# Second layer's u and gate projections: the hi weights meet hi and lo activations in one 512-column product

## The chip, the cores and the metric

One core of a Trainium2 chip runs the whole program. The metric is the device time of one execution in microseconds (us), as the median of several runs. TensorE (PE) does the matrix products, and the loads of its stationary operand are shown apart as PEld. VectorE (DVE), ScalarE (ACT) and GpSimd (POOL) do the elementwise work, and the queues of SyncE (SP) and ACT issue the DMAs.

## What is computed

Two residual layers over 256 positions of width 2048. The first is a bidirectional RWKV-7 mixer and is untouched here. The second is a gated spatial unit; cut to what matters:

```python
def chunked_sgu_mixer(h, w_in, ln_g, ln_b, w_s, b_s, w_out):
    u, v, gate = jnp.split(h @ w_in, 3, axis=-1)      # h: 256 x 2048, each part 4096 wide
    u = jax.nn.gelu(u)
    v = layer_norm(jax.nn.gelu(v), ln_g, ln_b)
    vc = v.reshape(Bsz, T // CHUNK, CHUNK, G_GROUPS, G_GROUP_W)
    s = jnp.einsum('gij,bcjgd->bcigd', w_s, vc) + b_s.T[:, :, None]
    s = s.reshape(Bsz, T, BRANCH)
    return (u * s * jax.nn.silu(gate)) @ w_out
```

The result is added to the input, and a final RMS norm closes the trunk.

## The kernel before

Every large product is made of three products of the type fp32r: both operands are split into a rounded part (hi) and the rest (lo), and hi·hi, hi·lo and lo·hi are summed in PSUM; lo·lo is left out. The function `mm3` (lines 159 to 163) issues the three: line 161 takes the first operand's hi and the second's hi, line 162 hi and lo, line 163 lo and hi.

Weights come from HBM in pieces of 128 x 1024 (512 KB). `convert` (lines 129 to 148) issues the DMA on SP's queue into a raw tile, ACT casts it to hi (line 146), and DVE subtracts to get lo (line 147). There are three hi and three lo tiles, so piece n+3 can be cast only when PE is through with piece n. `fetch` keeps up to three pieces converted ahead. The order in which each engine then runs its instructions is set by a scheduler when the program is built, from the program order and a simulated timeline.

The second layer has three stages:

- the v stage (lines 1008 to 1023): stationary are 128 x 128 blocks of the activations z1, moving are 512 columns of weights;
- the stage of u and gate, 16 groups of 256 channels (the loop from line 1033): here the weights are stationary and the activations move. For each of 16 k-blocks and 2 channel blocks `project` (lines 175 to 188) calls `mm3` with 256 columns (all positions): 192 products a group, 96 for u and 96 for gate. u and gate have one PSUM bank each (`ua`, `ga`), with both channel blocks side by side;
- the output stage (lines 1069 to 1095), with stationary blocks of the gated result (`zh_o1`, `zl_o1`, `bh_o1`, `bl_o1`) and 512 moving columns of weights. Its last eight pieces lie in tiles called `end`, which take over the place of z1.

In the group loop DVE multiplies the accumulated u by the RMS factor `rb2` (line 1041) and ACT takes its gelu (line 1042); DVE multiplies the gate likewise (line 1045), ACT takes a tanh into `Gt` (line 1046), DVE makes the SiLU from it (line 1047), and POOL multiplies it into U (line 1048). `Ga` and `Gt` have one buffer each. DVE also normalises the v columns of the group (lines 1055 to 1057), PE mixes them by four 128-column products (`sgu`, line 1061), and DVE and ACT put the result together and split it (lines 1063 to 1065 and `halve`). PSUM banks are handed out by `bank` (lines 791 to 793) in pairs, in turn from the tags acc and pg, with two banks each.

Of the kernel before, what the change touches and what calls it, by code (L numbers as in the profile page):

```python
# [11 lines left out]
F32R = mybir.dt.float32r  # L12
AF = mybir.ActivationFunctionType
ALU = mybir.AluOpType
# [8 lines left out]
def trunk(tc, x, norm_g, final_norm_g, w_in, mu_prev, mu_next, w0, w_up, a0, a_up, k_k, k_a, r_k,  # L23
          ln_w, ln_b, w_out, g_w_in, g_ln_g, g_ln_b, g_w_s, g_b_s, g_w_out, out):
    nc = tc.nc
    V, S, G, PE = nc.vector, nc.scalar, nc.gpsimd, nc.tensor
    P = 128
    T = x.shape[1]
    D = x.shape[2]
    KT = D // P  # L30
# [25 lines left out]
    def sm(name, tag="pg", bufs=2):  # L56
        return psm.tile([P, 512], F32, tag=tag, name=name, bufs=bufs)
# [92 lines left out]
    def prefetch():  # L150
        while queue and len(ready) < 3:
            ready.append(convert(*queue.popleft()))

    def fetch():

        prefetch()
        return ready.popleft()

    def mm3(acc, a, b, first, last):

        PE.matmul(acc, a[0], b[0], start=first, stop=False, skip_group_check=True)  # L161
        PE.matmul(acc, a[0], b[1], start=False, stop=False, skip_group_check=True)  # L162
        PE.matmul(acc, a[1], b[0], start=False, stop=last, skip_group_check=True)  # L163

    def run(steps):
        for _ in steps:
            pass
# [7 lines left out]
    def project(width, accs, zT):  # L175


        m = width // len(accs)
        k = 0
        while k < KT:  # L180
            n, hi, lo = fetch()
            for j in range(n):
                for i, acc in enumerate(accs):
                    cs = slice(i * m, (i + 1) * m)
                    mm3(acc, (hi[:, j, cs], lo[:, j, cs]), (zT[0][:, k], zT[1][:, k]),
                        k == 0 and i % 2 == 0, k == KT - 1)
                k += 1
                yield

# [19 lines left out]
    with tc.tile_pool(name="pr", bufs=6) as pr:  # L209
        groups, cur, n = [], [], 0  # L210
        for name, a in plist:
            if n + a.shape[0] > P:
                groups.append(cur)
                cur, n = [], 0
# [3 lines left out]
        for gi, grp in enumerate(groups):  # L218
            if gi == 1:
                prefetch()  # L220
            n = sum(a.shape[0] for _, a in grp)
# [47 lines left out]
    for k in range(DK, KT, 4):  # L269
        cs = slice(k * P, (k + 4) * P)  # L270
# [64 lines left out]
    for todo in plan:  # L335
        for s, b in todo:
# [3 lines left out]
            else:  # L340
                want_cols(w_in, segment[s] + b * 2 * P, 2 * P, f"w{s}{b}_")
    run(project(NL * P, laccs, zT))

    def low_rank():
# [70 lines left out]
    def mains(todo, st):  # L415
        slot = dict(k=0, r=4, g=12, v=8) if "k" in dict(todo) else dict(v=0, g=4)
        last = -4
        for s, b in todo:
            if s == "u":
                st[b]["wu"] = fetch()  # L420
                continue
            last = max(last + 4, slot[s])
            yield last * MT
            acc = acc_pair(f"acc{s}{b}")
            for i, _ in enumerate(project(2 * P, [acc[:, 0], acc[:, 1]], zT)):
                yield last * MT + i * dt
            if s == "g":
                SG = fr.tile([P, 2, T], F32, tag="SG", name=f"SG{b}", bufs=2)
                S.activation(SG, acc, AF.Tanh, scale=0.5)
                V.scalar_tensor_tensor(SG, SG, 1.0, acc, ALU.add, ALU.mult)  # L430
                st[b]["SG"] = SG
            elif s == "v":
                Vt = fr.tile([P, 2, T], F32, tag="Vt", name=f"Vt{b}", bufs=2)
                shifted(acc, Vt, b, 2)
                st[b]["Vt"] = Vt
            else:
                t = fr.tile([P, 2, T], F32, tag=f"{s}t", name=f"{s}t{b}")
                shifted(acc, t, b, dict(r=0, k=1)[s])
                st[b][dict(r="Rt", k="Kt")[s]] = t
        if ("g", NB - 1) in todo:  # L440
            yield 12 * MT
            for i, _ in enumerate(early_first()):
                yield 12 * MT + i
# [347 lines left out]
    def bank(name):  # L791
        banks[0] += 1
        return sm(name, ("acc", "pg")[(banks[0] - 1) // 2 % 2])

    def out_banks(m, name):
        return [bank(f"{name}{m}_{tt}") for tt in range(TT)]

    def halve(o, e0, n, src):

        S.mul(o[0][:, e0:e0 + n], src, 0.5)  # L800
        V.scalar_tensor_tensor(o[1][:, e0:e0 + n], src, 0.5, o[0][:, e0:e0 + n].bitcast(F32), ALU.mult, ALU.subtract)
# [100 lines left out]
    hp = top.enter_context(tc.tile_pool(name="hp", bufs=1, reuse_waits="tile"))  # L902
# [14 lines left out]
    ends = []  # L917

    def end_tiles(i):

        if not ends:
            ends.extend(hp.tile([P, KT, T], F32R, tag=f"z1{t}", name=f"end{t}").rearrange("p k t -> p (k t)")
                        .rearrange("p (e m) -> p e m", m=512) for t in "hl")
        return [t[:, 2 * i:2 * i + 2] for t in ends]

    wv = g_w_out.rearrange("(e p) m -> p e m", p=P)
    for i in range(LAST // 2):
        e = NCT - LAST + 2 * i
        want(wv[:, e:e + 2, (NM - 1) * 512:NM * 512], 2, 512, f"pe{e}", partial(end_tiles, i))
# [10 lines left out]
        o = oA if e < HE else oB  # L940
        return [t[:, e % HE:e % HE + n] for t in o]

    z1 = [hp.tile([P, KT, T], F32R, tag=f"z1{t}", name=f"z1{t}") for t in "hl"]
    part1 = hp.tile([P, TT, NM], F32, name="part1")
    def residual(m):

# [38 lines left out]
    rb2 = rb.unsqueeze(1).to_broadcast([P, 2, T])  # L985
# [17 lines left out]
    def vcols(tt, c, n):  # L1003
        return vn[c // (E // 2)][:, tt, c % (E // 2):c % (E // 2) + n]
# [3 lines left out]
    for n in range(nst):  # L1008
        accs = out_banks(n, "vacc")
        k = 0  # L1010
        while k < KT:
            m, hi, lo = fetch()
# [15 lines left out]
    V.tensor_scalar(vrs, vmv[:, :, 1], LN_EPS, None, ALU.add)  # L1028
    G.tensor_tensor(vrs, vrs, halfpow[:, :TT], ALU.pow)

    pA = [zp.tile([P, HE, T], F32R, tag=t, name=f"{t}_o1") for t in ("zh", "zl")]
    pB = None
    for g in range(NG):
        if g == NG // 2:
            pB = [op.tile([P, HE, T], F32R, tag="bh", name="bh_o1"), hp.tile([P, HE, T], F32R, name="bl_o1")]
        U = gt.tile([P, 2, T], F32, tag="U", name=f"U{g}")
        Ga = gt.tile([P, 2, T], F32, tag="Ga", bufs=1, name=f"Ga{g}")
        Gt = gt.tile([P, 2, T], F32, tag="Gt", bufs=1, name=f"Gt{g}")
        ua = bank(f"uacc{g}").rearrange("p (i t) -> p i t", i=2)
        run(project(256, [ua[:, 0], ua[:, 1]], z1))  # L1040
        V.tensor_tensor(U, ua, rb2, ALU.mult)
        S.activation(U, U, AF.Gelu_apprx_tanh)
        ga = bank(f"gacc{g}").rearrange("p (i t) -> p i t", i=2)
        run(project(256, [ga[:, 0], ga[:, 1]], z1))
        V.tensor_tensor(Ga, ga, rb2, ALU.mult)
        S.activation(Gt, Ga, AF.Tanh, scale=0.5)
        V.scalar_tensor_tensor(Gt, Gt, 1.0, Ga, ALU.add, ALU.mult)
        G.tensor_tensor(U, U, Gt, ALU.mult)
        gb = gt.tile([P, 2, 256], F32, tag="gb", name=f"gb{g}")
        nc.scalar.dma_start(gb[:, 0], g_ln_g[0, g * 256:(g + 1) * 256].partition_broadcast(P))  # L1050
        nc.scalar.dma_start(gb[:, 1], g_ln_b[0, g * 256:(g + 1) * 256].partition_broadcast(P))
        with tc.issue_after(latest[0].ins), tc.issue_after(latest[1].ins):
            for tt in range(TT):
                vs = vcols(tt, g * 256, 256)
                V.tensor_scalar(vs, vs, vmv[:, tt, 0:1], vrs[:, tt:tt + 1], ALU.subtract, ALU.mult)
                V.tensor_tensor(vs, vs, gb[:, 0], ALU.mult)
                V.tensor_tensor(vs, vs, gb[:, 1], ALU.add)
        sp = sm(f"sgu{g}", ("pf", "pq")[g % 2], 1).rearrange("p (n i) -> p n i", i=P)
        for cl in range(2):
            for tt in range(TT):  # L1060
                PE.matmul(sp[:, cl * TT + tt], vcols(tt, g * 256 + cl * P, P), wsT[:, g], start=True, stop=True)
        s1 = gt.tile([P, 4, P], F32, tag="s1", bufs=1, name=f"s1_{g}")
        V.tensor_tensor(s1, sp, bsb[:, g:g + 1].to_broadcast([P, 4, P]), ALU.add)
        V.tensor_tensor(s1, s1, U.rearrange("p l (t i) -> p (l t) i", i=P), ALU.mult)
        halve(pA if g < NG // 2 else pB, 2 * g % HE, 2, s1.rearrange("p (l t) i -> p l (t i)", l=2))
# [3 lines left out]
    for m in range(NM):  # L1069
        accs = out_banks(m, "oacc1_")  # L1070
# [9 lines left out]
        for tt in range(TT):  # L1080

            ts_ = slice(tt * P, (tt + 1) * P)
            for e in range(e1, NCT):
                oh, ol = o1(e)
                _, hi, lo = rest[(e - e1) // 2]
                mm3(accs[tt], (oh[:, ts_], ol[:, ts_]), (hi[:, e % 2], lo[:, e % 2]), e == 0, e == NCT - 1)
        parts = 1 if m < NM - 1 else 2
        for tt in range(TT):
            for i in range(parts):
                cs = slice(i * (512 // parts), (i + 1) * (512 // parts))  # L1090
# [5 lines left out]
    for tt in range(TT):  # L1096
        rstd2 = rms(total(part2[:, tt:tt + 1], f"ssq2_{tt}", hp), f"rstd2_{tt}", hp, V)
        for m in range(NM):
            h = h1[m][:, tt]
# [37 lines left out]
```

## Time and profile before

| what | value |
|---|---|
| median of 3 runs | 2262.61 us (2259.36 to 2264.06) |
| the profiled execution's own time | 2260.96 us |
| its span, first to last instruction | 2259.2 us |
| PE busy, PEld busy | 2210.5 us (98%), 2013.8 us (89%) |
| DVE, ACT, POOL busy | 1601.3 us (71%), 1389.6 us (62%), 197.4 us (9%) |
| chain that ended last | PE 80%, ACT 8%, DVE 4%, DMA 4%, waits for nothing shown 2% |
| mean granted TensorE clock | 0.992 of full speed |

The duration of a matmul row is its whole way through the array. Matmuls overlap, so what a product costs in a dense stretch is the distance between the starts of two that follow each other, read from the timeline.

### The profile page before, as it was taken

How to read it: one execution, taken by the hardware profiler on the slowest of the kernel's cores; microseconds unless marked ns; L12 is line 12 of the kernel's file. 1: busy time of each engine (PE TensorE's matmuls, PEld its weight loads, DVE VectorE, ACT ScalarE, POOL GpSimd, SP SyncE). 2: the span in 40 equal slices, each digit the busy share in tenths (PEclk: the TensorE clock that was granted, in tenths of full speed). 3: DMA queues.
4: the chain of work that ended last, by engine and by line, in shares of the span. 5: the costliest groups of instructions: out<-in, count | busy, mean ns of one | idle time of the engine just before them, and what ended most of it. 6: DMA issues, size and time to landing. Idle time of an engine off the chain costs nothing.

```text
span 2259.2 us, 50510 instructions
## 1 busy us (share of the span) xinstructions
PE 2210.5 (98%) x21008; PEld 2013.8 (89%) x21008; DVE 1601.3 (71%) x3057; ACT 1389.6 (62%) x2128; POOL 197.4 (9%) x230
## 2 busy tenths in 40 slices
PE   7999999999999999999999999999999999999998
PEld 7898899999999999999999977878889999999886
DVE  5798789778877977887797774465556676676444
ACT  6657777777868777786877774464444444444343
POOL 2220101011111101001110100000000000000000
PEclk9999899999999999999999999999999999999999
DMA  5444234343343344434333455576776666665554
GB/s 167 133 131 136 65 114 123 97 126 117 101 134 107 110 119 125 118 102 130 107 116 117 145 175 171 194 250 193 222 206 188 186 185 189 187 187 189 199 194 156
DMA packets 286135, 339.36 MB, mean 150 GB/s; under 512 B 11600, under 2 KB 233552, under 8 KB 285776
## 3 DMA queue, kind: packets, MB, share of 16 engines
q1 hardware_dynamic: 265648, 314.88, 45.9%
q10 hardware_dynamic: 20256, 21.24, 3.2%
q8 instruction: 165, 2.70, 0.5%
q14 instruction: 66, 0.54, 0.1%
HBM read 329.78 MB, written 6.29 MB: 149 GB/s over the span
## 4 chain that ended last, share of the span: by engine, by line
PE 80%; ACT 8%; DVE 4%; DMA 4%; issue 2%; POOL 0%; SPq 0%; ACTq 0%; POOLq 0%; DVEq 0%
PE oacc L162 4%; PE oacc L163 4%; PE oacc L161 4%; PE gp L557 4%; PE accv L161 3%; PE accg L161 3%; PE uacc L161 3%; PE gacc L163 3%; PE gacc L161 3%; PE gacc L162 3%; PE uacc L162 3%; PE uacc L163 3%; PE accg L163 3%; PE accg L162 3%; PE vacc L163 3%; PE vacc L162 3%
## 5 line engine op out<-in xcount | busy, mean ns | idle before, releaser
L161 PE MATMUL accv<-zh,whi_wv 128*128 128x256 f32 x512 | 153.4, 300 | 2.2 <-ACT whi_wv L146 2.2
L163 PE MATMUL accg<-zh,wlo_wg 128*128 128x256 f32 x512 | 151.3, 295 | 0.5 <-DVE wlo_wg L147 0.5
L161 PE MATMUL acck<-zh,whi_wk 128*128 128x256 f32 x512 | 150.4, 294 | 1.2 <-ACT whi_wk L146 1.2
L163 PE MATMUL acck<-zh,wlo_wk 128*128 128x256 f32 x512 | 148.7, 290 | 2.8 <-DVE wlo_wk L147 2.8
L163 PE MATMUL accv<-zh,wlo_wv 128*128 128x256 f32 x512 | 148.8, 291 | 1.3 <-DVE wlo_wv L147 1.2
L163 PE MATMUL accr<-zh,wlo_wr 128*128 128x256 f32 x512 | 149.2, 291 | 0.6 <-DVE wlo_wr L147 0.6
L162 PE MATMUL accr<-zl,whi_wr 128*128 128x256 f32 x512 | 148.7, 290 | 0.0
L161 PE MATMUL accr<-zh,whi_wr 128*128 128x256 f32 x512 | 148.3, 290 | 0.0
L161 PE MATMUL accg<-zh,whi_wg 128*128 128x256 f32 x512 | 148.0, 289 | 0.0
L162 PE MATMUL accv<-zl,whi_wv 128*128 128x256 f32 x512 | 147.3, 288 | 0.0
L162 PE MATMUL acck<-zl,whi_wk 128*128 128x256 f32 x512 | 147.2, 287 | 0.0
L162 PE MATMUL accg<-zl,whi_wg 128*128 128x256 f32 x512 | 146.4, 286 | 0.0
L162 PE MATMUL uacc<-z1l,whi_u 128*128 128x256 f32 x512 | 146.1, 285 | 0.0
L163 PE MATMUL uacc<-z1h,wlo_u 128*128 128x256 f32 x512 | 146.0, 285 | 0.0
L161 PE MATMUL uacc<-z1h,whi_u 128*128 128x256 f32 x512 | 144.9, 283 | 0.0
L161 PE MATMUL gacc<-z1h,whi_g 128*128 128x256 f32 x512 | 144.9, 283 | 0.0
L162 PE MATMUL gacc<-z1l,whi_g 128*128 128x256 f32 x512 | 144.9, 283 | 0.0
L163 PE MATMUL gacc<-z1h,wlo_g 128*128 128x256 f32 x512 | 144.9, 283 | 0.0
L146 ACT CAST whi_g<-raw_g 128x1024 fp32r<-128x1024 f32 x64 | 67.1, 1048 | 114.0 <-PE uacc L162 73.7
L147 DVE TENSOR_TENSOR wlo_v<-raw_v,whi_v 128x1024 fp32r<-128x1024 f32 x64 | 78.4, 1225 | 80.4 <-ACT whi_v L146 80.4
L610 DVE TENSOR_TENSOR TD<-La,X 128x126 f32<-128x126 f32 (+22 forms) x496 | 126.8, 256 | 10.5
L147 DVE TENSOR_TENSOR wlo_u<-raw_u,whi_u 128x1024 fp32r<-128x1024 f32 x64 | 93.8, 1465 | 56.6 <-ACT whi_u L146 56.6
(333 smaller groups left out, 7307.3 us busy)
## 6 DMA issues: line engine op xcount, KB each, us to landing
raw_wk<-in_rwkv_w_in_dram SPq DMA_DIRECT2D x64, 512.0 KB, 3.9
raw_wr<-in_rwkv_w_in_dram SPq DMA_DIRECT2D x64, 512.0 KB, 3.7
raw_wv<-in_rwkv_w_in_dram SPq DMA_DIRECT2D x64, 512.0 KB, 3.7
raw_wg<-in_rwkv_w_in_dram SPq DMA_DIRECT2D x64, 512.0 KB, 3.7
raw_o<-in_rwkv_w_out_dram SPq DMA_DIRECT2D x64, 512.0 KB, 4.0
raw_v<-in_gmlp_w_in_dram SPq DMA_DIRECT2D x64, 512.0 KB, 4.3
raw_u<-in_gmlp_w_in_dram SPq DMA_DIRECT2D x64, 512.0 KB, 3.6
raw_g<-in_gmlp_w_in_dram SPq DMA_DIRECT2D x64, 512.0 KB, 3.6
```

The costliest lines, as they stand in the source:

```text
L146: latest[0] = S.copy(hi, raw)
L147: latest[1] = V.tensor_tensor(lo, raw, hi.bitcast(F32), ALU.subtract)
L161: PE.matmul(acc, a[0], b[0], start=first, stop=False, skip_group_check=True)
L162: PE.matmul(acc, a[0], b[1], start=False, stop=False, skip_group_check=True)
L163: PE.matmul(acc, a[1], b[0], start=False, stop=last, skip_group_check=True)
L557: PE.matmul(gp[h][:, c].rearrange("p q t -> p (q t)"), BK[H[h], d, cl, c].rearrange("p q t -> p (q t)"), AR[H[h], d, cl, c].rearrange("p q ...
L610: V.tensor_tensor(tv, La[:, j, 0:j].unsqueeze(2).to_broadcast([P, j, n]), X[:, j:j + 1, m:].to_broadcast([P, j, n]), ALU.mult)
```

## The change

The hi and lo parts of z1 lie side by side in one tile `zc` of shape (128, 16, 2, 256), at the place and in the room that the two tiles had. A new `project_wide` takes, for each k-block and channel block, one 512-column product of the hi weights with hi and lo activations (line 200 of the changed kernel) and one 256-column product of the lo weights with the hi activations (line 202). Each channel block gets a PSUM bank of its own: the left half sums hi·hi and lo·hi, the right half hi·lo. At the end `gated` copies the right half to `tmp` (= `Gt`) on ACT, adds the left half on DVE, and multiplies by `rb2`. The v stage and the end tiles use views of the new tile.

```diff
+    def project_wide(width, accs, zc):
+        m = width // len(accs)
+        k = 0
+        while k < KT:
+            n, hi, lo = fetch()
+            for j in range(n):
+                for i, acc in enumerate(accs):
+                    cs = slice(i * m, (i + 1) * m)
+                    PE.matmul(acc.rearrange("p h t -> p (h t)"), hi[:, j, cs], zc[:, k].rearrange("p h t -> p (h t)"),
+                              start=k == 0, stop=False, skip_group_check=True)
+                    PE.matmul(acc[:, 0], lo[:, j, cs], zc[:, k, 0], start=False, stop=k == KT - 1,
+                              skip_group_check=True)
+                k += 1
+                yield
...
-    z1 = [hp.tile([P, KT, T], F32R, tag=f"z1{t}", name=f"z1{t}") for t in "hl"]
+    zc = hp.tile([P, KT, 2, T], F32R, tag="z1", name="z1")
+    z1 = [zc[:, :, i] for i in range(2)]
...
+    def gated(name, dst, tmp):
+        acc = [bank(f"{name}_{i}").rearrange("p (h t) -> p h t", h=2) for i in range(2)]
+        run(project_wide(256, acc, zc))
+        for i in range(2):
+            S.copy(tmp[:, i], acc[i][:, 1])
+            V.tensor_tensor(dst[:, i], acc[i][:, 0], tmp[:, i], ALU.add)
+        V.tensor_tensor(dst, dst, rb2, ALU.mult)
...
-        ua = bank(f"uacc{g}").rearrange("p (i t) -> p i t", i=2)
-        run(project(256, [ua[:, 0], ua[:, 1]], z1))
-        V.tensor_tensor(U, ua, rb2, ALU.mult)
+        gated(f"uacc{g}", U, Gt)
         S.activation(U, U, AF.Gelu_apprx_tanh)
-        ga = bank(f"gacc{g}").rearrange("p (i t) -> p i t", i=2)
-        run(project(256, [ga[:, 0], ga[:, 1]], z1))
-        V.tensor_tensor(Ga, ga, rb2, ALU.mult)
+        gated(f"gacc{g}", Ga, Gt)
         S.activation(Gt, Ga, AF.Tanh, scale=0.5)
```

How it moves instructions, at three places. On PE, the passage from the gate of group 2 to u of group 3 in the kernel before (the last three products of the one and the first three of the other):

```order
L161 MATMUL gacc2_21553<-z1h_19184,whi_g2_12_21586 128x256
L162 MATMUL gacc2_21553<-z1l_19185,whi_g2_12_21586 128x256
L163 MATMUL gacc2_21553<-z1h_19184,wlo_g2_12_21587 128x256
L161 MATMUL uacc3_21700<-z1h_19184,whi_u3_0_21616 128x256
L162 MATMUL uacc3_21700<-z1l_19185,whi_u3_0_21616 128x256
L163 MATMUL uacc3_21700<-z1h_19184,wlo_u3_0_21617 128x256
```

and in the changed kernel:

```order
L200 MATMUL gacc2_0_21417<-z1_19184,whi_g2_12_21443 128x512
L202 MATMUL gacc2_0_21417<-z1_19184,wlo_g2_12_21444 128x256
L200 MATMUL gacc2_1_21418<-z1_19184,whi_g2_12_21443 128x512
L202 MATMUL gacc2_1_21418<-z1_19184,wlo_g2_12_21444 128x256
L200 MATMUL uacc3_0_21537<-z1_19184,whi_u3_0_21465 128x512
L202 MATMUL uacc3_0_21537<-z1_19184,wlo_u3_0_21466 128x256
```

Three products of 256 columns became one of 512 and one of 256, with a bank for each channel block; the stages before and after, and the places of the sgu products, stand on PE as they did.

On ACT, around the end of u and of the gate in group 3, before:

```order
L146 CAST whi_g3_4_21793<-raw_g3_4_21791 128x1024
L800 ACTIVATE zh_o1_20885<-s1_2_21692 128x512
L146 CAST whi_g3_8_21826<-raw_g3_8_21824 128x1024
L1042 ACTIVATE U3_21697<-U3_21697 128x512
L146 CAST whi_g3_12_21856<-raw_g3_12_21854 128x1024
L146 CAST whi_u4_0_21886<-raw_u4_0_21884 128x1024
L146 CAST whi_u4_4_21916<-raw_u4_4_21914 128x1024
L146 CAST whi_u4_8_21973<-raw_u4_8_21971 128x1024
L1046 ACTIVATE Gt3_21699<-Ga3_21698 128x512
L146 CAST whi_u4_12_22003<-raw_u4_12_22001 128x1024
```

and in the changed kernel:

```order
L817 ACTIVATE zh_o1_20884<-s1_2_21529 128x512
L1054 COPY Gt3_21536<-uacc3_0_21537 128x256
L146 CAST whi_g3_8_21637<-raw_g3_8_21635 128x1024
L1054 COPY Gt3_21536<-uacc3_1_21538 128x256
L146 CAST whi_g3_12_21659<-raw_g3_12_21657 128x1024
L1067 ACTIVATE U3_21534<-U3_21534 128x512
L146 CAST whi_u4_0_21681<-raw_u4_0_21679 128x1024
L146 CAST whi_u4_4_21703<-raw_u4_4_21701 128x1024
L1054 COPY Gt3_21536<-gacc3_0_21633 128x256
L146 CAST whi_u4_8_21757<-raw_u4_8_21755 128x1024
L1054 COPY Gt3_21536<-gacc3_1_21634 128x256
L146 CAST whi_u4_12_21779<-raw_u4_12_21777 128x1024
```

The first copy stands ahead of the third cast of the next stage, the second behind it; the tanh comes after the fourth cast and after the two DMA issues of a later group's `gb`.

On DVE, around the end of the gate in group 3, before:

```order
L147 TENSOR_TENSOR wlo_u4_4_21917<-raw_u4_4_21914,whi_u4_4_21916 128x1024
L1055 TENSOR_SCALAR vn_bh_19643<-vn_bh_19643,vmv_20879,vrs_20882 128x256 x2
L1056 TENSOR_TENSOR vn_bh_19643<-vn_bh_19643,gb3_21948 128x256
L1045 TENSOR_TENSOR Ga3_21698<-gacc3_21823,rb_19639 128x512
L1056 TENSOR_TENSOR vn_bh_19643<-vn_bh_19643,gb3_21948 128x256
L1057 TENSOR_TENSOR vn_bh_19643<-vn_bh_19643,gb3_21948 128x256
L147 TENSOR_TENSOR wlo_u4_8_21974<-raw_u4_8_21971,whi_u4_8_21973 128x1024
L1057 TENSOR_TENSOR vn_bh_19643<-vn_bh_19643,gb3_21948 128x256
L1047 SCALAR_TENSOR_TENSOR Gt3_21699<-Gt3_21699,Ga3_21698 128x512
L147 TENSOR_TENSOR wlo_u4_12_22004<-raw_u4_12_22001,whi_u4_12_22003 128x1024
```

and in the changed kernel:

```order
L1079 TENSOR_TENSOR vn_bh_19642<-vn_bh_19642,gb3_21731 128x256
L1055 TENSOR_TENSOR Ga3_21535<-gacc3_0_21633,Gt3_21536 128x256
L1079 TENSOR_TENSOR vn_bh_19642<-vn_bh_19642,gb3_21731 128x256
L1080 TENSOR_TENSOR vn_bh_19642<-vn_bh_19642,gb3_21731 128x256
L147 TENSOR_TENSOR wlo_u4_8_21758<-raw_u4_8_21755,whi_u4_8_21757 128x1024
L1055 TENSOR_TENSOR Ga3_21535<-gacc3_1_21634,Gt3_21536 128x256
L1080 TENSOR_TENSOR vn_bh_19642<-vn_bh_19642,gb3_21731 128x256
L1056 TENSOR_TENSOR Ga3_21535<-Ga3_21535,rb_19638 128x512
L147 TENSOR_TENSOR wlo_u4_12_21780<-raw_u4_12_21777,whi_u4_12_21779 128x1024
L1070 SCALAR_TENSOR_TENSOR Gt3_21536<-Gt3_21536,Ga3_21535 128x512
```

The first add stands where the multiplication stood, ahead of the third subtraction of the next stage; the second add and the multiplication stand between the third and the fourth, and the SiLU step has gone behind the fourth. SP's 638 rows and POOL's 221 rows keep their order.

## Rows read from the trace of the kernel before

**Rows 1.** The page's part 1: engine, busy us, share of the span, instructions.

```profile
PE 2210.5 (98%) x21008; PEld 2013.8 (89%) x21008; DVE 1601.3 (71%) x3057; ACT 1389.6 (62%) x2128; POOL 197.4 (9%) x230
```

**Rows 2.** Busy time by stretch: v stage, u and gate stage, output stage.

```profile
core 0: us, PE busy (x) PEld busy (x) DVE busy (x) ACT busy (x) POOL busy (x), PEclk, DMA share, GB/s
...
1514.50:1691.80 177.30, 177.30 (x795) 146.67 (x795) 91.08 (x86) 83.64 (x94) 0.70 (x1) 1.00 0.70 205
1691.80:2073.80 382.00, 382.00 (x3194) 381.96 (x3194) 259.31 (x316) 160.97 (x176) 20.16 (x16) 1.00 0.62 187
2073.80:2259.20 185.40, 177.22 (x778) 144.88 (x776) 93.07 (x96) 74.88 (x88) 2.39 (x3) 0.99 0.54 183
```

**Rows 3.** Groups by line: count | busy us, mean ns | idle before, releaser.

```profile
L161 PE MATMUL uacc<-z1h,whi_u 128*128 128x256 f32 x512 | 144.9, 283 | 0.0
L163 PE MATMUL gacc<-z1h,wlo_g 128*128 128x256 f32 x512 | 144.9, 283 | 0.0
L163 PEld LDWEIGHTS gacc<-z1h,wlo_g 128*128 128x128 f32 x512 | 98.3, 192 | 0.0
L146 ACT CAST whi_g<-raw_g 128x1024 fp32r<-128x1024 f32 x64 | 67.1, 1048 | 114.0 <-PE uacc L162 73.7 <-issue 40.3
```

**Rows 4.** Timeline of PE, u and gate stage: start us, us, engine, line, what.

```profile
1703.38 0.28 PE L161 MATMUL gacc<-z1h,whi_g 128*128 128x256 f32 x1
...
1714.90 0.28 PE L161 MATMUL uacc<-z1h,whi_u 128*128 128x256 f32 x1
...
1786.56 0.28 PE L163 MATMUL gacc<-z1h,wlo_g 128*128 128x256 f32 x1
1786.68 0.28 PE L161 MATMUL uacc<-z1h,whi_u 128*128 128x256 f32 x1
```

**Rows 5.** Timeline of PE, v stage, first and last of 22 matmuls.

```profile
1559.77 0.39 PE L162 MATMUL vacc<-wlo_v,z1h 128*128 128x512 f32 x1
...
1564.53 0.39 PE L163 MATMUL vacc<-whi_v,z1l 128*128 128x512 f32 x1
```

**Rows 6.** Timeline of PE, output stage's end tiles, first and last of 28 matmuls.

```profile
2239.65 0.40 PE L161 MATMUL oacc<-endh,bh_o 128*128 128x512 f32 x1
...
2245.95 0.40 PE L161 MATMUL oacc<-endh,bh_o 128*128 128x512 f32 x1
```

**Rows 7.** Groups by line: evacuations and adds of 128x256 and 128x512.

```profile
L689 ACT COPY Xs<-xp 128x256 f32<-128x256 f32 x64 | 23.5, 367 | 19.5 <-PE xp L684 18.7 <-DVE wlo_o L147 0.5
L709 DVE TENSOR_TENSOR SJ<-sp,SJ 128x256 f32<-128x256 f32 x32 | 13.4, 418 | 3.4 <-PE sp L700 3.4
L1041 DVE TENSOR_TENSOR U<-uacc,rb 128x512 f32<-128x512 f32 x16 | 11.1, 692 | 1.4 <-PE uacc L163 0.7
L1064 DVE TENSOR_TENSOR s<-s,U 128x512 f32<-128x512 f32 x16 | 11.0, 686 | 0.1
```

**Rows 8.** Timeline of DVE after the end of a gate (1786.84 us).

```profile
1787.08 0.68 DVE L1045 TENSOR_TENSOR Ga<-gacc,rb 128x512 f32<-128x512 f32 x1
...
1788.36 1.22 DVE L147 TENSOR_TENSOR wlo_u<-raw_u,whi_u 128x1024 fp32r<-128x1024 f32 x1
...
1790.76 2.27 DVE L147 TENSOR_TENSOR wlo_u<-raw_u,whi_u 128x1024 fp32r<-128x1024 f32 x1 [0.26 <-ACT whi_u L146]
...
1797.41 1.23 DVE L147 TENSOR_TENSOR wlo_g<-raw_g,whi_g 128x1024 fp32r<-128x1024 f32 x1 [1.33 <-ACT whi_g L146]
```

**Rows 9.** Timeline of POOL, the product of the same group.

```profile
1790.65 1.30 POOL L1048 TENSOR_TENSOR U<-U,Gt 128x512 f32<-128x512 f32 x1 [22.63 <-DVE Gt L1047]
```

**Rows 10.** Timeline of ACT's queue, the two DMA issues of one group's gb.

```profile
1789.94 0.33 ACTq L1050 DMA_DIRECT2D gb<-in_gmlp_ln_g_dram  x1
1790.30 0.46 ACTq L1051 DMA_DIRECT2D gb<-in_gmlp_ln_b_dram  x1
```

**Rows 11.** DMA issues of the u and gate stage: count, KB each, median us to landing.

```profile
raw_g<-in_gmlp_w_in_dram SPq DMA_DIRECT2D x63, 512.0 KB, 3.6
```

More of the change, by code (lines that the diff above doesn't have):

```diff
@@ L921, in end_tiles @@
         if not ends:
-            ends.extend(hp.tile([P, KT, T], F32R, tag=f"z1{t}", name=f"end{t}").rearrange("p k t -> p (k t)")
-                        .rearrange("p (e m) -> p e m", m=512) for t in "hl")
+            end = hp.tile([P, KT, 2, T], F32R, tag="z1", name="end").rearrange("p k h t -> p (k h t)")
+            ends.extend(end[:, i * KT * T:(i + 1) * KT * T].rearrange("p (e m) -> p e m", m=512) for i in range(2))
         return [t[:, 2 * i:2 * i + 2] for t in ends]
```

## The prediction

> **What bounds the kernel now.** First the page's shares [rows 1]: PE is busy 98% of the span, but a busy PE only says that some matmul is in flight, so I went on to the stretches [rows 2]. The change lies in the second of them, 382.0 us long. There PE is never idle, PEld is busy 381.96 us, DVE 68% and ACT 42%, and the granted clock is 1.00, which is the 2.4 GHz level. Then the groups by line [rows 3]: the idle time before the products of u and gate is 0.0, while ACT's casts spent 73.7 us waiting for PE to free a weight tile. So PE waits for nobody, and the conversion of weights waits for PE. In such a stage a product costs the distance to the start of the next, not its own duration of 283 ns. That distance I took from the timeline of PE [rows 4]: 96 gate products lie between 1703.38 and 1714.90, 120.0 ns each.
>
> **The price of a 512-column product.** The stage shows none, so it comes from the nearest dense stretch, the v stage [rows 5]: 22 matmuls, 21 distances, 4.76 us, 226.7 ns each. It is near in all that matters: the same type, the same two tiles read (weights and z1, only with their roles exchanged), an LDWEIGHTS for each product, the clock at 1.00. The two prices fit a straight line: 106.7 ns for 256 more columns, 0.417 ns a column, and 13.3 ns that each product costs whatever its width.
>
> So a k-block and channel block cost 3 x 120.0 = 360.0 ns before, and 226.7 + 120.0 = 346.7 ns after. Columns are the same (768); one product fewer saves its fixed 13.3 ns. There are 16 k-blocks x 2 blocks x 2 (u, gate) x 16 groups = 1024 of them: **1024 x 13.3 = 13.65 us less**. The rest of a group is the sgu products: three groups take 1786.68 - 1714.90 = 71.78 us [rows 4], 23.93 each, of which 192 x 0.120 = 23.04 are u and gate. The other 0.89 us stays, so a group should take 23.08 us and the stage 368.4.
>
> Bounds of the 512-column price. Above, 240 ns, as much as two 256-column products: nothing gained. A row on the way there: the last pieces of the output stage [rows 6], 27 distances in 6.30 us, 233.3 ns, so operands in other places of SBUF do cost more, and the gain would be 6.8 us. Below, the columns alone, 213.3 ns by the slope of the two prices, which would gain 27.3 us. I take 226.7, since the row with the same two tiles is the nearest, and z1 and the weights keep their places.
>
> The trace has a fixed cost of 13.3 ns a product. The Trainium skill, TensorE: Matmul & The Clock Gate, section Back-to-back issue gap, has the warm distance as N / 2.4 plus about 2.5 ns, so that one product fewer would be worth 2.5 ns, and the sum, as an estimate, 1024 x 2.5 = 2.6 us, which could not be told from no change. It speaks against this change; its 109 ns for 256 columns and 216 ns for 512 stand against the trace's 120.0 and 226.7, and I follow the trace.
>
> **What is added.** ACT gets 64 copies of 128x256 out of PSUM, 64 x 0.367 = 23.5 us, and DVE 64 adds of that size with one operand in PSUM, 64 x 0.418 = 26.8 us [rows 7]. The 32 multiplications stay, from SBUF instead of PSUM (0.686 against 0.692 us). ACT's load becomes 161.0 + 23.5 = 184.5 us and DVE's 259.3 + 26.8 = 286.1 us, in a stage of 368 us: 50% and 78%. Neither becomes the bound, and what counts is whether a weight tile comes late.
>
> The place with least room is the end of a gate, 1786.84 us in the group I read. The subtraction for the third piece of the next u ends at 1788.36 + 1.22 = 1789.58 [rows 8]; that piece is due after two pieces of 24 x 0.120 = 2.88 us, near 1792.5, some 2.9 us later. After the change a copy (0.37) goes ahead of its cast, and an add of 0.42 stands ahead of it on DVE where a multiplication of 0.68 stood: some 0.1 us later in all. The fourth piece gets the other add and the multiplication in front of its subtraction, about 1.1 us; it began at 1790.76 and took 2.27 us while POOL's product ran [rows 8, 9], ended at 1793.03, and is due near 1796.2 (8.64 us of the three pieces and 0.89 of sgu after 1786.68), so 2 us remain. The tanh now comes behind two DMA issues, 0.33 + 0.46 us [rows 10], and POOL's product comes later by about 1.5 us with it and the later SiLU step. What waits for that product is the merge with sgu, 2 us further on, and the next u's copy into the single `Gt`, 11.1 us after the gate's end, while the product ended 5.1 us after it (1790.65 + 1.30). So all additions cost nothing: the cover is PE's own stream with two converted pieces (5.5 us) in hand. Without it, each 0.1 us of late weights at all 32 stage ends would cost 3.2 us.
>
> Banks: u and gate now take two each, all four in every group, so the pair of u is needed again after the gate's 11.1 us. The last add of u should end some 3 us into that time. The DMAs keep their order on SP; weights have to come 3.7% faster, and a transfer lands in 3.6 us [rows 11] with the DMA engines at 62% [rows 2]. Nothing in the v stage or the output stage moves.
>
> **The sum.** The profiled execution took 2260.96 us, 1.65 under the median of 2262.61. Less 13.65 it is 2247.3; on the scale of the median **2249.0 us**, 0.6% less. A measurement of this kernel can tell about 0.2%, 4.5 us, from no change.
>
> **Rivals.**
>
> *Nothing to speak of is gained.* The fixed cost isn't one of each instruction: in the stage of u and gate PEld is busy all the time, in the v stage 147 of 177 us [rows 2], so the 13.3 ns may have two causes that merely look alike, and a 512-column stream of z1 against stationary weights may pay near 240 ns. Against it: one line through both prices, with a v stage that has room in PEld. Time: 1024 x 0 saved, 2262.6. The skill's distance, above, falls here with 2260.0. Chance 8%.
>
> *More is gained.* The fixed cost is the wait for a weight load and hides behind the longer product: 226.7 + 106.7 = 333.4 ns, 27 us less, 2235.4. For it: PEld's full load. Against it: in the v stage PEld has room and the 13.3 ns are there all the same. Chance 5%.
>
> *Weights come late.* If copies (0.74), adds and multiplication (1.53), DMA issues (0.79) and POOL's slowing of one more subtraction (2.27 - 1.22 = 1.05) all fell into one chain ahead of the fourth subtraction after a gate, it would be 4.1 us late with 3.2 us in hand (1793.03 to 1796.2): 0.9 us of PE's time at 16 gate ends, 14.4 us, which eats the gain: 2263.4. It decides when PE waits 13.65 / 16 = 0.85 us at each. For it: DVE at 78%, in lumps. Against it: DVE and ACT are idle 32% and 58% of the stage now [rows 2], and most additions fall there. Chance 3%.
>
> *Slower: the weight load comes into the open.* A load takes 192 ns from start to end [rows 3], while products start every 120 ns, so loads overlap with more than one product. If the load for the lo product, pulled ahead during the 512 columns, held the place of the next, then the next hi load could start only with the lo product and would have only its 107 ns of columns over it: the 256-column slot would cost 192 instead of 120 ns, in each of 1024 pairs. 1024 x (226.7 + 192 - 360) = 60.1 us slower, 2322.7. It decides at a slot over 360 - 226.7 = 133.3 ns. For it: PEld has nothing to spare in this stage. Against it: today the same 192 ns lie over products of 256 columns alone, without a wait. Chance 4%.
>
> **How the numbers follow.** Forecast 80%, rivals 8, 5, 3 and 4%. The forecast's own range: upwards, the 233.3 ns of the end tiles, 6.8 us less, 2255.8, and the 1.45 us by which the slowest run lies over the median, 2257; downwards, the 3.25 us by which the fastest lies under it, and a quarter of the second rival's effect on the 256-column slot, 1024 x 3.3 ns = 3.4 us, 2242. The four rivals lie outside; they are the 2 in 10 left out. Faster by over 0.2%: the forecast and the second rival, 85%; within 0.2%: the first and the third, 11%; slower: 4%.
>
> **What would show it.** Right: 226 to 227 ns from a 512-column product to the 256-column one behind it and 120 ns from that to the next; groups of 23.1 us; the stage 368 us; no idle time before these products; copies near 0.37 us and adds near 0.42 us; v and output stage as they were. The first rival shows as 235 ns or more from a 512-column product on, the second as 107 ns after a 256-column one, the third as idle time of PE that a subtraction to lo ends, at the fourth piece after a gate, the fourth as 192 ns after a 256-column product. Wrong for another reason I would be if a stage that the change doesn't touch became longer, or if PE waited at the start of u for the banks or for ACT's copies.

## The result and the profile after

The changed kernel takes **2250.3 us** in the median of 4 runs (2248.06 to 2250.95), the kernel before, on the same chip, 2261.45 us (4 runs, 2259.36 to 2264.06). The ratio is 0.9948 with a 95% interval of 0.9931 to 0.9966: 0.5% faster, where 0.6% was forecast (2249.0 us, range 2242 to 2257).

The page's part 1, its rows of the new lines, and the stretches of the changed kernel (its u and gate stage begins at 1694.20):

```profile
PE 2200.9 (98%) x19984; PEld 1959.1 (87%) x19984; DVE 1611.2 (72%) x3121; ACT 1406.3 (63%) x2192; POOL 181.0 (8%) x230
...
L200 PE MATMUL uacc<-z,whi_u 128*128 128x512 f32 x512 | 179.0, 394 | 0.0
L200 PE MATMUL gacc<-z,whi_g 128*128 128x512 f32 x512 | 177.3, 393 | 0.0
...
L202 PE MATMUL uacc<-z,wlo_u 128*128 128x256 f32 x512 | 142.4, 284 | 0.0
L202 PE MATMUL gacc<-z,wlo_g 128*128 128x256 f32 x512 | 140.2, 279 | 0.0
```

```profile
core 0: us, PE busy (x) PEld busy (x) DVE busy (x) ACT busy (x) POOL busy (x), PEclk, DMA share, GB/s
1516.90:1694.20 177.30, 177.30 (x795) 146.68 (x794) 91.03 (x86) 83.42 (x94) 0.70 (x1) 1.00 0.70 205
1694.20:2063.80 369.60, 369.60 (x2170) 325.48 (x2169) 268.97 (x378) 178.46 (x239) 20.07 (x16) 1.00 0.63 193
2063.80:2249.20 185.40, 177.15 (x777) 144.82 (x776) 93.18 (x98) 75.23 (x90) 2.40 (x3) 0.98 0.56 183
```

Against [rows 1, 2]: PE has 1024 products fewer, the u and gate stage went from 382.00 to 369.60 us, and the stages behind and ahead of it are as long as they were (177.30 and 185.40). PE is never idle in that stage, and no idle time stands before a product of u or gate, as in [rows 3]. The span fell by 10.0 us and not by 12.4, because the first layer came out 2.4 us longer in this execution (the v stage starts at 1516.90, before at 1514.50). That is no part of the change: in the repeat of the same kernel below the u and gate stage starts 3.2 us earlier and is equally long.

The start and the end of one gate on PE, from the timeline; the first row is the first gate product, the last row the first product of the next u:

```profile
1751.82 0.39 PE L200 MATMUL gacc<-z,whi_g 128*128 128x512 f32 x1
...
1762.58 0.39 PE L200 MATMUL gacc<-z,whi_g 128*128 128x512 f32 x1
1762.81 0.27 PE L202 MATMUL gacc<-z,wlo_g 128*128 128x256 f32 x1
1762.92 0.40 PE L200 MATMUL uacc<-z,whi_u 128*128 128x512 f32 x1
```

The 32 pairs of the gate take 1762.92 - 1751.82 = 11.10 us, 347 ns a pair (one product of 512 and one of 256 columns), where the same passage took 11.52 us [rows 4]. In the last pair shown 0.23 us lie behind the 512 columns and 0.11 us behind the 256.

What was added, from the groups by line in the u and gate stage, and the passage on DVE behind a gate that ends at 1786.1:

```profile
L1055 DVE TENSOR_TENSOR U<-uacc,Gt 128x256 f32<-128x256 f32 x32 | 13.5, 422 | 2.1 <-ACT Gt L1054 0.7
L1055 DVE TENSOR_TENSOR Ga<-gacc,Gt 128x256 f32<-128x256 f32 x30 | 12.5, 418 | 0.0
L1054 ACT COPY Gt<-uacc 128x256 f32<-128x256 f32 x32 | 12.0, 374 | 16.6 <-PE uacc L202 16.6
L1054 ACT COPY Gt<-gacc 128x256 f32<-128x256 f32 x31 | 11.5, 372 | 23.0 <-PE gacc L202 23.0
```

```profile
1786.62 0.42 DVE L1055 TENSOR_TENSOR Ga<-gacc,Gt 128x256 f32<-128x256 f32 x1
1786.96 0.42 DVE L1079 TENSOR_TENSOR vn_bh<-vn_bh,gb 128x256 f32<-128x256 f32 x1
1787.29 0.42 DVE L1080 TENSOR_TENSOR vn_bh<-vn_bh,gb 128x256 f32<-128x256 f32 x1
1787.62 1.22 DVE L147 TENSOR_TENSOR wlo_u<-raw_u,whi_u 128x1024 fp32r<-128x1024 f32 x1
1788.76 0.42 DVE L1055 TENSOR_TENSOR Ga<-gacc,Gt 128x256 f32<-128x256 f32 x1
...
1790.03 1.22 DVE L147 TENSOR_TENSOR wlo_u<-raw_u,whi_u 128x1024 fp32r<-128x1024 f32 x1
```

The copies wait for the last products of their group, as they should; nobody on PE waits for them. The fourth subtraction after the gate ends at 1791.25. Its piece is due after three pieces of 8 pairs and the sgu products, 24 x 0.347 + 0.93 = 9.3 us after 1786.1, at 1795.4, so 4 us are in hand.

### The profile page after: what moved, and what is told of

Same layout as the page of the kernel before. It is cut to its first block, busy times and chain, and to the rows that moved or that the text cites. A ratio compares the mean times of both kernels' runs of the same rounds, so it can differ in the third digit from the quotient of the medians.

```text
span 2249.2 us, 48589 instructions
## 1 busy us (share of the span) xinstructions
PE 2200.9 (98%) x19984; PEld 1959.1 (87%) x19984; DVE 1611.2 (72%) x3121; ACT 1406.3 (63%) x2192; POOL 181.0 (8%) x230
## 4 chain that ended last, share of the span: by engine, by line
PE 76%; ACT 10%; DMA 6%; DVE 5%; issue 3%; POOL 0%; ACTq 0%; POOLq 0%; SPq 0%; DVEq 0%
PE uacc L200 5%; PE gacc L200 5%; PE oacc L162 4%; PE oacc L161 4%; PE oacc L163 4%; PE gp L574 4%; PE gacc L202 3%; PE uacc L202 3%; PE vacc L161 3%; PE vacc L162 3%; PE vacc L163 3%; PE accv L161 3%; PE accg L161 2%; PE accg L163 2%; PE accg L162 2%
## 5 line engine op out<-in xcount | busy, mean ns | idle before, releaser
L200 PE MATMUL uacc<-z,whi_u 128*128 128x512 f32 x512 | 179.0, 394 | 0.0
L200 PE MATMUL gacc<-z,whi_g 128*128 128x512 f32 x512 | 177.3, 393 | 0.0
L202 PE MATMUL uacc<-z,wlo_u 128*128 128x256 f32 x512 | 142.4, 284 | 0.0
L202 PE MATMUL gacc<-z,wlo_g 128*128 128x256 f32 x512 | 140.2, 279 | 0.0
L629 DVE TENSOR_TENSOR X<-X,TD 128x126 f32<-128x126 f32 (+22 forms) x496 | 125.0, 252 | 9.4
L147 DVE TENSOR_TENSOR wlo_o<-raw_o,whi_o 128x1024 fp32r<-128x1024 f32 x64 | 78.0, 1223 | 74.6 <-ACT whi_o L146 74.3
L147 DVE TENSOR_TENSOR wlo_p<-raw_p,whi_p 128x1024 fp32r<-128x1024 f32 x60 | 73.9, 1232 | 75.6 <-ACT whi_p L146 75.6
L146 ACT CAST whi_p<-raw_p 128x1024 fp32r<-128x1024 f32 x60 | 63.1, 1051 | 91.5 <-PE oacc L163 87.3
```

Source lines behind the costliest of these rows:

```text
L146: latest[0] = S.copy(hi, raw)
L147: latest[1] = V.tensor_tensor(lo, raw, hi.bitcast(F32), ALU.subtract)
L200: PE.matmul(acc.rearrange("p h t -> p (h t)"), hi[:, j, cs], zc[:, k].rearrange("p h t -> p (h t)"), start=k == 0, stop=False, skip_group_ ...
L202: PE.matmul(acc[:, 0], lo[:, j, cs], zc[:, k, 0], start=False, stop=k == KT - 1, skip_group_check=True)
L629: V.tensor_tensor(X[:, 0:j, m:], X[:, 0:j, m:], tv, ALU.add)
```

## The experiments

The theory is that each product has a fixed cost, and that the gain is that of 1024 products fewer. Its rivals: the new layout of z1, the separate banks or the copies have a part in the time, or a weight load sets a floor. Four kernels went to the chip together, with 24 runs of the kernel before (median 2261.15).

**Three products again, all else as changed.**

```diff
-                    PE.matmul(acc.rearrange("p h t -> p (h t)"), hi[:, j, cs], zc[:, k].rearrange("p h t -> p (h t)"),
-                              start=k == 0, stop=False, skip_group_check=True)
+                    for h in range(2):
+                        PE.matmul(acc[:, h], hi[:, j, cs], zc[:, k, h],
+                                  start=k == 0 and h == 0, stop=False, skip_group_check=True)
```

> The changed kernel with its 512-column product cut in two of 256 columns (hi weights with hi activations, hi weights with lo activations); tile, banks, copies and adds stay as changed. If the gain is one of the number of products (13.3 ns for each that is left out), the pair costs 3 x 120 = 360 ns again, the u and gate stage 382 us, the time that of the kernel before, ratio 1.000 (+-0.002). If banks, copies and adds cost something, the stage comes out over 382 us and the ratio over 1.002. If the gain came from the layout or the banks, the stage stays near 369.6 us and the ratio near 0.995.

Measured: 2260.52 us (11 runs), ratio 0.9998 (0.9989 to 1.0007). Its u and gate stage:

```profile
1689.60:2071.50 381.90, 381.90 (x3193) 381.87 (x3192) 266.46 (x378) 177.83 (x239) 19.99 (x16) 1.00 0.62 187
```

The stage is that of before although DVE and ACT carry the added work (266.46 against 259.31 us, 177.83 against 160.97). So the whole gain hangs on the two products that became one, and banks, copies and adds cost nothing. A product left out takes its weight load with it (PEld has as many instructions as PE in [rows 1] and in the page after); which of the two the fixed cost belongs to, no run here separates.

**The new layout alone**, in the kernel before: `zc` with its two views and the `end` tile, and `project` as it was.

```diff
...
-    z1 = [hp.tile([P, KT, T], F32R, tag=f"z1{t}", name=f"z1{t}") for t in "hl"]
+    zc = hp.tile([P, KT, 2, T], F32R, tag="z1", name="z1")
+    z1 = [zc[:, :, i] for i in range(2)]
```

> The kernel before with the tile of the change alone: hi and lo of z1 side by side, products, banks and evacuation as before. No theory gives the layout a price: stage 382 us, ratio 1.000 (+-0.002). If the place of the activations had a part in the gain, the stage would be shorter than 381 us.

Measured: 2262.41 us (11 runs), ratio 1.0008 (0.9999 to 1.0017), the stage 382.00 us. The place of hi and lo does nothing by itself.

**Without copies and adds.** The right half of each bank is left out of u and gate.

```diff
-            S.copy(tmp[:, i], acc[i][:, 1])
-            V.tensor_tensor(dst[:, i], acc[i][:, 0], tmp[:, i], ALU.add)
-        V.tensor_tensor(dst, dst, rb2, ALU.mult)
+            V.tensor_tensor(dst[:, i], acc[i][:, 0], rb2[:, i], ALU.mult)
```

> The changed kernel without the sum of the halves: the copies and adds are left out, and the left half alone is multiplied by the RMS factor (hi times lo is left out of u and gate). If copies and adds are hidden, the stage takes 369.6 us as in the changed kernel and the ratio to the kernel before stays at 0.995. If the 1.2 us by which the stage missed the forecast 368.4 are theirs, it takes 368.4 us and the ratio falls to about 0.994.

Measured: 2255.25 us (8 runs), ratio 0.9973 (0.9963 to 0.9983). There is less work, and yet the kernel is some 5 us slower than the changed one. The stage, and nine pairs of a gate on PE:

```profile
1694.60:2069.50 374.90, 374.90 (x2170) 327.02 (x2169) 247.27 (x347) 159.69 (x176) 34.51 (x16) 1.00 0.62 191
```

```profile
1729.66 0.40 PE L200 MATMUL gacc<-z,whi_g 128*128 128x512 f32 x1
1729.90 0.28 PE L202 MATMUL gacc<-z,wlo_g 128*128 128x256 f32 x1
...
1732.84 0.40 PE L200 MATMUL gacc<-z,whi_g 128*128 128x512 f32 x1
```

3.18 us for nine pairs, 353 ns each and not 347, with PE busy throughout and the clock at 1.00: the products themselves follow each other more slowly. That fits neither side of what was expected, and it became the open question.

**All hi products of a k-block before its lo products.**

```diff
-                    PE.matmul(acc[:, 0], lo[:, j, cs], zc[:, k, 0], start=False, stop=k == KT - 1,
-                              skip_group_check=True)
+                for i, acc in enumerate(accs):
+                    cs = slice(i * m, (i + 1) * m)
+                    PE.matmul(acc[:, 0], lo[:, j, cs], zc[:, k, 0], start=False, stop=k == KT - 1,
+                              skip_group_check=True)
```

> The changed kernel with the order of the products changed: for each k-block first the 512-column products of both channel blocks, then the two 256-column ones. If a product costs by its columns and a fixed part, the order doesn't matter: stage 368.4 to 369.6 us, ratio 0.995. If the distances of 231 ns behind a 512-column product and 116 to 117 behind a 256-column one come from the alternation, a 512-column product behind another shows about 227 ns and a 256-column one behind another about 120, and the stage loses up to 1 us.

Measured: 2250.88 us (5 runs), ratio 0.9956 (0.9943 to 0.9968), the stage 370.20 us. A 512-column product behind another did not come to 227 ns, nor a 256-column one behind another to 120: over the stage the means are 233 and 115 ns. So the immediate alternation of widths is not what the gain or the uneven split of a pair hangs on.

Two kernels have one run each, beside one run of the kernel before, of 2260.92 us. They differ from it by far more than its runs differ among themselves.

**The lo product with 512 columns too** (this adds lo·lo, which the kernel before leaves out).

```diff
-                    PE.matmul(acc[:, 0], lo[:, j, cs], zc[:, k, 0], start=False, stop=k == KT - 1,
-                              skip_group_check=True)
+                    PE.matmul(acc.rearrange("p h t -> p (h t)"), lo[:, j, cs], zc[:, k].rearrange("p h t -> p (h t)"),
+                              start=False, stop=k == KT - 1, skip_group_check=True)
```

> The changed kernel with the lo weights too meeting hi and lo activations in 512 columns (lo times lo is added to the sum). By the line through the prices of the kernel before, the second product costs 226.7 instead of 120.0 ns: 106.7 x 1024 = 109 us more than the changed kernel, stage about 478 us, every distance near 227 ns. If a 512-column product of moving activations over stationary weights costs the 231 ns that the changed kernel shows behind it, every distance is 231 ns and the stage takes about 487 us.

Measured: 2359.59 us, the stage 478.10. From PE's timeline, 43 distances:

```profile
1746.24 0.39 PE L200 MATMUL gacc<-z,whi_g 128*128 128x512 f32 x1
...
1755.99 0.39 PE L202 MATMUL uacc<-z,wlo_u 128*128 128x512 f32 x1
```

They take 9.75 us, 226.7 ns each, which is the price that was taken from the v stage [rows 5]. z1 moving against stationary weights costs nothing extra here.

**The hi product cut into 384 and 128 columns.**

```diff
...
+                    for c0_, c1_ in ((0, 384), (384, 512)):
+                        PE.matmul(acc.rearrange("p h t -> p (h t)")[:, c0_:c1_], hi[:, j, cs],
+                                  zc[:, k].rearrange("p h t -> p (h t)")[:, c0_:c1_],
+                                  start=k == 0 and c0_ == 0, stop=False, skip_group_check=True)
```

> The changed kernel with its 512-column product cut into 384 and 128 columns of the same hi weights: as many products as before the change, and as many columns. If a product costs 13.3 ns and 0.417 ns a column, the three cost 173.3 + 66.7 + 120.0 = 360 ns and the stage 382 us, as with three of 256. If a weight load sets a floor of about 110 ns on each product (the sgu products of 128 columns come 109 to 112 ns apart), the 128-column one costs about 110 instead of 66.7: 403 ns, 44 us more, stage about 426 us.

Measured: 2308.84 us, the stage 429.80, with the same columns and the same number of products as before. Two rounds on PE (the first row of each holds the 384 and the 128 columns):

```profile
1729.78 0.40 PE L201 MATMUL uacc<-z,whi_u 128*128 128x384 f32 x2
1730.02 0.33 PE L204 MATMUL uacc<-z,wlo_u 128*128 128x256 f32 x1
1730.19 0.41 PE L201 MATMUL uacc<-z,whi_u 128*128 128x384 f32 x2
...
1730.60 0.40 PE L201 MATMUL uacc<-z,whi_u 128*128 128x384 f32 x2
```

A round takes 0.41 us where the line through the two prices gives 0.36; over the stage it is 47.8 us more than the 382.0 of three equal products, 46.7 ns in each of 1024 rounds. The loads of the weights in the same stretch (the second row holds two):

```profile
1729.55 0.19 PEld L204 LDWEIGHTS uacc<-z,wlo_u 128*128 128x128 f32 x1
1729.66 0.31 PEld L201 LDWEIGHTS uacc<-z,whi_u 128*128 128x128 f32 x2
```

In the whole stage no load starts less than 108 ns after the one before it, while the product of 128 columns has the next one only 60 ns behind it. The excess shows one product later: the distance behind the 256-column product is 0.17 us (1730.02 to 1730.19) instead of 0.12. That fits the second theory of the expectation, a floor under each weight load of about 110 ns, which put the stage near 426 us. A weight load can thus come into the open, as the fourth rival had it, but by this floor and not at that rival's 192 ns; and it took a product shorter than the floor, which the change does not have.

**What makes a pair cost 353 or 347 ns?** The distances between the products in the traces answered half of it without a run. They come in two kinds of pattern that repeat as long as nothing comes between: 232, 118, 241, 120, 235, 114 ns (three pairs in 1060, 353.3 a pair), and 230, 113, 232, 118, 231, 112, 233, 117 or plain 230, 117 (346.5 to 347 a pair). Below they are called the long and the short pattern. The first gate of the changed kernel shows both, with a place between them (1711.09) where the scheduler had put two hi products ahead of their two lo products:

```profile
1710.03 0.40 PE L200 MATMUL gacc<-z,whi_g 128*128 128x512 f32 x1
...
1711.09 0.63 PE L200 MATMUL gacc<-z,whi_g 128*128 128x512 f32 x2
1711.56 0.39 PE L202 MATMUL gacc<-z,wlo_g 128*128 128x256 f32 x2
1711.79 0.40 PE L200 MATMUL gacc<-z,whi_g 128*128 128x512 f32 x1
...
1712.83 0.39 PE L200 MATMUL gacc<-z,whi_g 128*128 128x512 f32 x1
```

Three pairs take 1.06 us ahead of it and 1.04 behind. In the changed kernel every gate has such a place, at k = 8; in the kernel without copies and adds the scheduler put none into any gate. So that experiment had changed the order on PE too. Three kernels tested it, with 8 runs of the kernel before (median 2261.13).

**Without copies and adds, with the order of the changed kernel's gates**, then **the changed kernel with one more such place in each gate (k = 12)**, and **the changed kernel once more, unaltered**. The first two have the same edit, with k = 8 and k = 12; `swap` lists the k-blocks that are issued hi, hi, lo, lo, and is empty for u:

```diff
...
+                together = k in swap
                 for i, acc in enumerate(accs):
...
-                    PE.matmul(acc[:, 0], lo[:, j, cs], zc[:, k, 0], start=False, stop=k == KT - 1,
-                              skip_group_check=True)
+                    if not together:
+                        PE.matmul(acc[:, 0], lo[:, j, cs], zc[:, k, 0], start=False, stop=k == KT - 1,
+                                  skip_group_check=True)
+                for i, acc in enumerate(accs):
+                    if together:
+                        PE.matmul(acc[:, 0], lo[:, j, i * m:(i + 1) * m], zc[:, k, 0], start=False,
+                                  stop=k == KT - 1, skip_group_check=True)
...
+        run(project_wide(256, acc, zc, (8,) if name[0] == "g" else ()))
```

> As no_halves_sum (the copies and the adds of halves left out, the products of hi weights with lo activations missing from the output), but in every gate group the pairs of k = 8 are issued hi, hi, lo, lo, which is how the changed kernel's gate groups stand in the program; in no_halves_sum they stood hi, lo, hi, lo. In the traces so far the distances inside a run of pairs come in two repeating patterns that keep themselves up: 232/118/241/120/235/114 (three pairs 1060 ns, 353.3 a pair: all of no_halves_sum) and 230/113/232/118/231/112/233/117 or 230/117 (346.5 to 347 a pair: most of the changed kernel), and they were seen to swap only where a hi, hi, lo, lo stands or the norm's products are put between. Theory 'pattern': the reordered pairs swap the gate groups to the short pattern; the gate group falls from 11.30 us to 11.1-11.2, the stage from 374.8 us to 369.5-372.5. Rival 'traffic': the longer distances come from what ACT and DVE no longer do on the PSUM banks; then the gate group stays at 11.30 and the stage at 374.5-375.

Measured: 2250.44 us (4 runs), ratio 0.9950 (0.9934 to 0.9967). The stage and one gate:

```profile
1693.00:2064.90 371.90, 371.90 (x2169) 325.51 (x2168) 245.86 (x347) 159.56 (x176) 33.95 (x16) 1.00 0.62 192
```

```profile
1750.80 0.40 PE L201 MATMUL gacc<-z,whi_g 128*128 128x512 f32 x1
...
1762.02 0.40 PE L201 MATMUL uacc<-z,whi_u 128*128 128x512 f32 x1
```

The stage fell by 3.0 us against the kernel without copies and adds, with two neighbouring products exchanged in each gate and no work changed. Each gate went from 11.30 to 11.22 us, which in 16 gates is less than half of it; the rest came in the u behind it, where the short pattern goes on. The rival that blamed the traffic of ACT and DVE expected no change, and has fallen for these 3.0 us. The 2.4 us that are still missing against the changed kernel's 369.5 were not tested. In this trace an exchange in each u, ahead of the sgu products, brings the long pattern back, and about half of the pairs run in it; in the changed kernel that exchange stands between the sgu products, and the short pattern stays.

> The changed kernel with one more place in every gate group (k = 12) where the pairs are issued hi, hi, lo, lo. In the changed kernel's first u group such a place was seen to turn the short pattern into the long one, in its first gate group the long into the short. Theory 'pattern': the added place may turn the last 6 pairs of the gate group and the first 14 to 16 of the next u group to the long pattern, 20 x 6.7 ns = 0.13 us a group, 2 us in the stage: 371 to 372 instead of 369.6, the kernel 2 us slower than the changed one; at most 375 if the pattern then stays. If the place changes only within the short patterns, 369 to 370. Rival 'traffic': the stage stays at 369.6 within 0.3, the copies and adds being all there.

Measured: 2254.13 us (5 runs), ratio 0.9968 (0.9955 to 0.9981), the stage:

```profile
1696.70:2068.40 371.70, 371.70 (x2170) 326.61 (x2169) 269.00 (x378) 178.04 (x239) 20.11 (x16) 1.00 0.62 192
```

It is 2.1 us longer than the changed kernel's, as the theory of the patterns had it (371 to 372).

> The changed kernel unaltered, beside the two others on one chip. Theory 'pattern': as the order of the products fixes the pattern, the stage repeats at 369.6 within 0.3 us with the same distances; median 2248 to 2252 us. Rival (the pattern falls by chance in each execution): a stage anywhere from 369 to 375.

Measured: 2250.75 us (4 runs), ratio 0.9950 (0.9935 to 0.9965), the stage:

```profile
1691.00:2060.50 369.50, 369.50 (x2169) 325.38 (x2168) 268.74 (x378) 178.24 (x239) 20.11 (x16) 1.00 0.63 193
```

The stage repeats within 0.1 us while the first layer's end moved by 3.2 us. With the same order of products the same pattern came again in a second execution, so nothing points to chance.

## Why the prediction was right, step by step

**A fixed cost for each product, 13.3 ns, saved 1024 times: right in kind and nearly in size.** Forecast for the stage 368.4 us, measured 369.6, so 12.4 of the 13.65 us came. With three products instead of two and all else as changed, nothing was left of it. The price of 226.7 ns from the v stage held where both products had 512 columns. The Trainium skill, TensorE: Matmul & The Clock Gate, section Back-to-back issue gap, gives the distance by which the gain would have been 2.6 us, as an estimate, for isolated matmuls and not for a stream in which each has its weight load, as here; the prediction did not say so. For this stream it is not borne out: 12.4 us were measured.

**The split of a pair, 226.7 + 120.0: wrong, its sum right.** In the stage the 512-column slot costs 231 to 232 ns and the 256-column one some 116. The gate's 11.10 us are 347 ns a pair against 346.7. What would have counted as a sign of the first rival, a distance of 235 ns or more, stood in the trace of the kernel without copies and adds, as part of the long pattern, and in the first group of the changed kernel too.

That the sum came out so well is in part luck. Nothing in the prediction knew of two patterns; in the long one, which the kernel without copies and adds kept almost throughout, the stage takes 374.9 us, and some 7 us of the 13.65 would have come. The price of 512 columns was also less settled than the prediction took it to be. Its end tiles, at 233.3 ns, were not the only dearer place in the trace of before: in the output stage the same width costs 226.7 ns with one pair of stationary tiles and 231.7 ns with the next (9 and 12 distances):

```profile
2226.28 0.39 PE L162 MATMUL oacc<-wlo_p,zh_o 128*128 128x512 f32 x1
...
2228.32 0.39 PE L163 MATMUL oacc<-whi_p,zl_o 128*128 128x512 f32 x1
...
2229.00 0.40 PE L162 MATMUL oacc<-wlo_p,bh_o 128*128 128x512 f32 x1
...
2231.78 0.40 PE L162 MATMUL oacc<-wlo_p,bh_o 128*128 128x512 f32 x1
```

The prediction put such a difference down to the operands' places in SBUF. The tiles do differ between these rows, but no run moves zh_o or bh_o with all else kept, so what sets the price there stays open.

**Where the missing 1.2 us are.** A steady group takes 12.04 (u and sgu) + 11.10 (gate) = 23.14 us, where 23.08 were forecast; in 15 groups that makes 15 x 0.06 = 0.9 us. The rest lies in the first group, which runs partly in the long pattern.

**Additions at no cost: right, though ACT's and DVE's load was put too high.** The copies took 0.373 us and the adds 0.42, as estimated. But DVE became busy for 269.0 us, not 286.1, ACT for 178.5, not 184.5. Two things were left out. Instructions that follow each other overlap: 0.42 us long, they start 0.33 us apart (1786.96, 1787.29, 1787.62). And POOL's product, forecast to come 1.5 us later, left the subtraction that it had run beside. That subtraction takes 1.22 us now and took 2.27 [rows 8]. The 62 subtractions of the u pieces show it in the groups by line of the stage, first of before:

```profile
L147 DVE TENSOR_TENSOR wlo_u<-raw_u,whi_u 128x1024 fp32r<-128x1024 f32 x62 | 91.3, 1473 | 53.6 <-ACT whi_u L146 53.6
```

and of the changed kernel:

```profile
L147 DVE TENSOR_TENSOR wlo_u<-raw_u,whi_u 128x1024 fp32r<-128x1024 f32 x62 | 75.7, 1221 | 47.7 <-ACT whi_u L146 47.7
```

POOL's product now runs beside a subtraction of a gate piece, and gives part of this back: the mean of those 64 went from 1223 to 1271 ns. The piece with least room had 4 us in hand instead of the 2 forecast.

**The rivals.** That nothing is gained is refuted by the stage. That more is gained did not come: the distance behind a 256-column product fell, to 116 and not to 106.7, and the one behind the 512 columns rose by about as much. Weights did not come late, as there is no idle time before a product of u or gate. Weight loads did not come into the open in this change; they did in the kernel with a product of 128 columns.

## What to carry to other kernels

In a stage that PE fills without a wait, read the price of a product as the distance between starts, at two widths, in the same trace, and in every dense stretch that it has: here one width cost 226.7, 231.7 and 233.3 ns in three of them. The part that doesn't grow with the columns is what merging products saves, so long as none of them becomes too short to cover the next weight load. An experiment that takes work off other engines can alter the order that a scheduler gives to PE: compare the order before blaming the work.

## What the runs showed that was not expected

- A stream of 512- and 256-column products settles into one of two kinds of repeating pattern, 353.3 or some 347 ns a pair, at the same clock. Exchanging two neighbouring products was seen to move the stream from one into the other. Between the kernel that keeps almost wholly to the long pattern and the changed one lie 5.3 us of this stage (374.9 against 369.6); exchanges in the gates alone brought back 3.0 of them. One width alone can have more than one price as well: 512 columns cost 226.7, 231.7 or 233.3 ns by the stretch, where 256 columns in the stage before cost 120.0 nearly throughout. Why there are such patterns, and what in an exchange or in a tile decides which one follows, was not found out.
- Weight loads never started less than 108 ns apart in the stage of the kernel cut into 384 and 128 columns. What a product of 128 columns leaves uncovered shows in the distance behind the next product: 0.17 us after a 256-column product that follows one of 128.
